# A decoder layer's out projection: two full token blocks first, the meta rows last

## The chip, the cores and the metric

One core of a Trainium2 chip runs one launch of the kernel. The metric is the device time of that launch in microseconds (us), median of several runs. Five engines work side by side and wait for each other by semaphores: PE (matrix products), DVE, ACT and POOL (elementwise work), and SP, which here only issues DMA transfers. Each engine takes its instructions in its own order; an instruction that waits holds up everything behind it on that engine.

## What is computed

One layer of a hybrid decoder on 1024 tokens and 16 meta rows put ahead of them, 1024 wide, all float32:

```python
a = rmsnorm(h, ln_mix_pre)                  # h = meta rows, then x
dq, dk, dv, hq, hf, hi, hg = split(a @ w_in)
y_diff = diff_attention(dq, dk, dv, ...)    # 4 heads
y_hgrn = hgrn2(hq, hf, hi, hg, ...)         # 4 heads, chunked recurrence
mix = concatenate([y_diff, y_hgrn]) @ w_out # the OUT PROJECTION, 1024 x 1024
h = h + rmsnorm(mix, ln_mix_post)
a = rmsnorm(h, ln_ffn_pre)
y = conv_ffn(a, w_ffn_up, ...)              # up, causal conv of width 3, gelu gate, down
h = h + rmsnorm(y, ln_ffn_post)
return h[16:]                               # the meta rows are dropped
```

Since the convolution looks back two rows, only the last two meta rows are needed behind the attention: "the meta rows" below are these two.

## The kernel before

Every float32 product is made of three products of rounded operands: each operand is split into a high part (a cast on ACT) and a low part (operand minus high part, on DVE or POOL), and PE adds high x high, high x low, low x high. So each step of the out projection is a group of three matmuls (`out_part`, L937, L939, L941).

**The out projection** is `mix @ w_out`. `mix` lies transposed in SBUF in eight pieces (k = 0 to 7) of 128 columns. The tokens are nine blocks: block 0 is the two meta rows (`tok(0)` gives 2 rows), blocks 1 to 8 have 128 each. `w_out` is taken in two halves of 512 columns: `load_wo(0)`, then `load_wo(1)`. A piece of a half is loaded as `wor` (256 KB, SP, L904) and split into `woh` (ACT) and `wol` (DVE or POOL).

*First half* (`out_first`, tags `py0_i`). PE runs it interleaved with the last HGRN head (`hgrn_head`), since the scores of that head give piece k = 7. `mix_split(i, k0, k1)` makes the parts of `mix` of block i in a tile `mm` (k 0 to 3 or 4 to 6), out of a pool `mixsplit` with two buffers a tag. It also writes the parts to a scratch tensor `msc` in DRAM (SP, L927), except for block 0. The half opens with blocks 0 and 1 in turn, two pieces of k each, goes on with block 2, and so on to 8; what PE sums is copied to `y0`. Piece k = 7 follows by itself when the head's rows are done (`out_last(p)`, PSUM tile `pz`): three matmuls, an add to `y0` on DVE, and the sum of squares of the row on ACT. ACT has to write the squares somewhere: for p < 3 they go into the PSUM tile `pz` itself. Blocks 0, 1, 2 get their `pz` at the end of `out_first`; 3 to 8 get it inside the second half, two behind each of its blocks 0, 1, 2.

*Second half* (the loop at the end, tags `py1_i`). The parts are not made again but read back from `msc` in four pieces of two k (`mix_load(i, c)`, tile `mp`, four buffers, 256 KB each, SP, L1001). Block 0 alone has no parts in `msc`: they are made anew from `mix` on ACT and DVE (four casts, four subtractions, L53). The order is block 0, 1, ..., 8. Behind each, `post(i, py)` adds the residual and makes the next norm, and two blocks later `trans(i)` transposes the rows on PE.

Three details matter. `gpo` and `gfb` are gain rows broadcast by SP (L1022, L1024), in a pool that is opened late. The **up weights** `ra` (`load_raw4`, L1106, 256 KB each, five buffers) are loaded for the next stage: `issue_after(wo0_loaded)` lets the scheduler put their issue anywhere behind the last load of the first half of `w_out`. Their splits `uh` (ACT), `ul` (POOL or DVE) and sums `ws` (POOL, L1110) follow. Last, every line of ACT and DVE of the helper that records the order is L53, so these are told apart by tiles.

Of the kernel before, what the change touches and what calls it, by code (L numbers as in the profile page):

```python
# [17 lines left out]
P = 128  # L18
# [8 lines left out]
NBLK = 9  # L27
# [58 lines left out]
def layer_kernel(ctx: ExitStack, tc: tile.TileContext, x, meta, table, lbl, gpre, gpost, win,  # L86
# [830 lines left out]

    def mix_split(pl, i, k0, k1):
        r, t0 = tok(i)
        m = pl.tile([P, 2, k1 - k0, P], F32R, tag="m1" if k1 - k0 == 1 else "mm", name=f"mm{i}_{k0}")  # L920
        src = mix(slice(k0, k1), t0, t0 + r)
        A.copy(m[:, 0, :, :r], src)
        V.tensor_tensor(m[:, 1, :, :r], src, m[:, 0, :, :r].bitcast(F32), op=ALU.subtract)
        if i:
            for c in range(k0 // 2, (k1 + 1) // 2):
                ka, kb = max(k0, 2 * c), min(k1, 2 * c + 2)
                SY.dma_start(msc[i, c][:, :, P * (ka - 2 * c):P * (kb - 2 * c)],  # L927
                             m[:, :, ka - k0:kb - k0].bitcast(F32).rearrange("p l k t -> p l (k t)"))
        return m, k0, k1, r
# [11 lines left out]
            T.matmul(py[:r], ml[:, j, :r], hi, start=False, stop=(last and k == k1 - 1))  # L941
            yield 216

    first_split = mix_split(map_, 0, 0, 4)
    wo0 = load_wo(0)
    wo0_loaded = last_load[-1]

    pre_last = {}

# [4 lines left out]
    def out_last(p):  # L954
        r = tok(p)[0]
        py = ps_in(f"pz{p}")
        yield from out_part(pre_last.pop(p), py, wo0, True, True)
        V.tensor_tensor(y0[:r, p], y0[:r, p], py[:r], op=ALU.add)
        junk = py if p < 3 else qp.tile([P, 512], F32, tag="junk", name=f"jz{p}", bufs=1)
        A.activation(junk[:r], y0[:r, p], AF.Square, accum_out=ssy[:r, p, 0:1])  # L960
        A.activation(ssy[:r, p, 0:1], ssy[:r, p, 0:1], AF.Identity, bias=eps[:r], scale=1.0 / D)
        if p < 3:
            y0_gain(p)

    def out_first():
        pys = [ps_in(f"py0_{i}") for i in range(2)]
        sps = [first_split, mix_split(map_, 1, 0, 4)]
        for ks in ((0, 1), (2, 3)):
            for i in range(2):
                yield from out_part(sps[i], pys[i], wo0, ks[0] == 0, False, ks)  # L970
        sqs = [mix_split(map_, i, 4, 7) for i in range(2)]
        for i in range(2):
            yield from out_part(sqs[i], pys[i], wo0, False, True)
            if i == 0:
                sp_ = mix_split(map_, 2, 0, 4)
            A.copy(y0[: tok(i)[0], i], pys[i][: tok(i)[0]])
        for i in range(2, NBLK):
            py = ps_in(f"py0_{i}")
            sq_ = mix_split(map_, i, 4, 7)
            yield from out_part(sp_, py, wo0, True, False)  # L980
            if i + 1 < NBLK:
                sp_ = mix_split(map_, i + 1, 0, 4)
            yield from out_part(sq_, py, wo0, False, True)
            (V.tensor_copy if i == NBLK - 1 else A.copy)(y0[: tok(i)[0], i], py[: tok(i)[0]])
        for p in range(3):
            while p not in finished:
                yield None
            if p < 2:
                for q in range(2 * p, min(2 * p + 2, 3)):
                    pre_last[q] = mix_split(map_, q, 7, 8)  # L990
            yield from out_last(p)
# [5 lines left out]
    def mix_load(i, c):  # L997
        r, t0 = tok(i)
        m = mlp.tile([P, 2, 2, P], F32R, tag="mp", name=f"mp{i}_{c}", bufs=4)
        if i:  # L1000
            SY.dma_start(m.bitcast(F32).rearrange("p l k t -> p l (k t)"), msc[i, c])  # L1001
        else:
            src = mix(slice(2 * c, 2 * c + 2), t0, t0 + r)
            A.copy(m[:, 0, :, :r], src)
            V.tensor_tensor(m[:, 1, :, :r], src, m[:, 0, :, :r].bitcast(F32), op=ALU.subtract)
# [21 lines left out]
    def post(i, py):  # L1027
        r, t0 = tok(i)
        xh = qp.tile([P, D], F32, tag="xh", name=f"xh{i}")
        SY.dma_start(xh[:r], meta[14:16, :] if i == 0 else x[P * (i - 1): P * i, :])  # L1030
        if i >= 3 and i % 2:
            a2 = mxp.tile([P, 8, 384], F32, tag="mix2", name=f"a2_{i}").rearrange("p a c -> p (a c)")[:, :D]
        else:
# [3 lines left out]
        s1, s2 = ssy[:r, i, 1:2], ssy[:r, i, 2:3]  # L1037
        A.activation(junk[:r], py[:r], AF.Square, accum_out=s1)
# [7 lines left out]
        A.activation(a2[:r], xh[:r], AF.Square, accum_out=s2)  # L1046
# [54 lines left out]
    def load_raw4(ft):  # L1101
        raws.clear()
        for nm, m, c in (("11", ft, 0), ("22", ft + NF, 1), ("21", ft + NF, 0), ("12", ft, 1)):
            raws[nm] = swp.tile([P, 512], F32, tag="ra", name=f"ra{ft}_{nm}", bufs=5)
            with tc.issue_after(wo0_loaded.ins):
                SY.dma_start(raws[nm], wup[m][:, 512 * c: 512 * (c + 1)])  # L1106

    def w_sum(nm, a, b, op):
# [38 lines left out]
            split(hi, lo, raws[nm], G)  # L1147
            plain[nm] = (hi, lo)

    ms = [mix_load(0, c) for c in range(4)]  # L1150
    for i in range(NBLK):
        py = ps_s(f"py1_{i}")[:, 0]
        if i == NBLK - 1:
            prep_plain()
        if i >= 3:
            y0_gain(i)
        nxt = []
        for c in range(4):
            if c == 2:
                if i < 3:  # L1160
                    for p in (3 + 2 * i, 4 + 2 * i):
# [15 lines left out]
        if i < 3:  # L1177
            for p in (3 + 2 * i, 4 + 2 * i):
                for _ in out_last(p):
                    pass  # L1180
    close(q_cm, ma_cm, y_cm, wo_cm)
# [368 lines left out]
```

## Time and profile before

| | |
|---|---|
| median of 3 runs (1350.4 to 1353.11) | 1351.55 us |
| the profiled execution | 1350.57 us |
| its span, first to last instruction | 1348.7 us |
| PE busy | 1297.8 us, 96% of the span |
| DVE, ACT, POOL busy | 927.7, 687.3, 422.1 us |
| mean granted clock of PE | 0.993 |
| first half of the out projection | 528.69 to 595.84 us |
| k = 7 parts and second half | 595.84 to about 669 us |

The profiled execution is 0.98 us under the median, and 1.87 us of it lie outside the span. Rows of the trace give the start in us from the span's first instruction, the duration, the engine, the line, out<-in, and in brackets how long the engine had been idle and what released it. "Waits" sums such idle time by what was waited for. PEclk is the share of the full TensorE clock that was granted.

### The profile page before, as it was taken

Reading aid. Unit: us, or ns where it says so; the run is one execution under the profiler, and the core shown is the slowest. Engines: PE = TensorE matmul, PEld = TensorE weight load, DVE = VectorE, ACT = ScalarE, POOL = GpSimd, SP = SyncE. Lnnn points to the kernel's source line nnn. Section 1 sums busy time; section 2 is a strip of 40 time slices with the busy share of each in tenths; the row PEclk is TensorE's granted clock in tenths of the full one; section 3 lists DMA queues with packets and bytes.
Section 4 is the critical chain, followed back from the end, with each engine's and each line's share of the span. In section 5 each row is a group of like instructions: output and inputs, shape, how many; then the busy total and the mean of one; then the engine's idle time right before and its main releaser. Section 6 shows DMA issues by size and latency. Waiting matters only on the chain.

```text
span 1348.7 us, 26259 instructions
## 1 busy us (share of the span) xinstructions
PE 1297.8 (96%) x10170; PEld 1187.0 (88%) x10170; DVE 927.7 (69%) x1599; ACT 687.3 (51%) x1629; POOL 422.1 (31%) x334
## 2 busy tenths in 40 slices
PE   6999999999999999989999999999999999999997
PEld 5899899989999997667798999999999998878875
DVE  7665657574746464756798787787777776697586
ACT  7465346534644664455674444444454444554453
POOL 3211211021112110234036656656656640010121
PEclk9999999999999999999999999999999999999999
DMA  6331333132311002648712222223222225955253
GB/s 213 113 126 52 103 126 102 44 127 102 103 44 42 26 23 85 218 145 261 262 40 87 94 87 72 79 88 102 79 87 78 72 89 185 339 186 169 87 203 117
DMA packets 87028, 157.01 MB, mean 116 GB/s; under 512 B 9796, under 2 KB 24164, under 8 KB 86903
## 3 DMA queue, kind: packets, MB, share of 16 engines
q1 hardware_dynamic: 86902, 155.33, 34.2%
q8 instruction: 80, 1.31, 0.4%
q14 instruction: 46, 0.37, 0.1%
HBM read 114.66 MB, written 40.63 MB: 115 GB/s over the span
## 4 chain that ended last, share of the span: by engine, by line
PE 69%; DVE 6%; DMA 4%; issue 3%; ACT 3%; POOL 1%; SPq 0%; DVEq 0%; ACTq 0%; POOLq 0%
PE pd L1396 5%; PE pd L1397 5%; PE pd L1395 5%; PE pb L1237 4%; PE pb L1239 4%; PE pb L1238 4%; PE pc L1237 3%; PE pc L1239 2%; PE pc L1238 2%; PE pa L1237 2%; PE pa L1238 2%; PE pa L1239 2%; PE pa L694 2%; PE py L937 2%; PE py L941 2%
## 5 line engine op out<-in xcount | busy, mean ns | idle before, releaser
L1237 PE MATMUL pb<-t,uh 128*128 128x258 f32 x504 | 143.5, 285 | 4.7 <-DVE u L53 4.7
L1239 PE MATMUL pb<-t,ul 128*128 128x258 f32 x504 | 141.7, 281 | 0.0
L1238 PE MATMUL pb<-t,uh 128*128 128x258 f32 x504 | 141.6, 281 | 0.0
L1396 PE MATMUL pd<-wl,gh 128*128 128x512 f32 x308 | 122.0, 396 | 0.6 <-DVE wl L53 0.5
L1395 PE MATMUL pd<-wh,gh 128*128 128x512 f32 x308 | 121.7, 395 | 0.0
L1397 PE MATMUL pd<-wh,gl 128*128 128x512 f32 x308 | 121.6, 395 | 0.0
L53 DVE SCALAR_TENSOR_TENSOR c<-uu,cwt,c 128x514 f32<-128x514 f32 (+1 forms) x88 | 96.4, 1096 | 20.6 <-ACT c L53 19.9
L1204 POOL TENSOR_TENSOR c<-c,c 128x514 f32<-128x514 f32 (+1 forms) x44 | 63.4, 1441 | 122.8 <-ACT c L53 120.1
L1237 PEld LDWEIGHTS pb<-t,uh 128*128 128x128 f32 x504 | 94.9, 188 | 6.8 <-DVE u L53 6.2
L1239 PEld LDWEIGHTS pb<-t,ul 128*128 128x128 f32 x504 | 95.2, 189 | 0.0
L1238 PEld LDWEIGHTS pb<-t,uh 128*128 128x128 f32 x504 | 95.2, 189 | 0.0
L1238 PE MATMUL pc<-t,uh 128*128 128x258 f32 (+1 forms) x336 | 95.1, 283 | 0.0
L1237 PE MATMUL pc<-t,uh 128*128 128x258 f32 (+1 forms) x336 | 95.0, 283 | 0.0
L1239 PE MATMUL pc<-t,ul 128*128 128x258 f32 (+1 forms) x336 | 95.0, 283 | 0.0
L1237 PE MATMUL pa<-t,uh 128*128 128x258 f32 (+1 forms) x336 | 94.8, 282 | 0.0
L1238 PE MATMUL pa<-t,uh 128*128 128x258 f32 (+1 forms) x336 | 94.6, 281 | 0.0
L1239 PE MATMUL pa<-t,ul 128*128 128x258 f32 (+1 forms) x336 | 94.2, 280 | 0.0
L53 DVE SCALAR_TENSOR_TENSOR c<-ug,cwt,c 128x514 f32<-128x514 f32 (+1 forms) x88 | 86.1, 978 | 2.7 <-ACT c L53 2.0
L145 POOL TENSOR_TENSOR ul<-ws,uh 128x512 fp32r<-128x512 f32 x42 | 60.0, 1428 | 42.9 <-ACT uh L53 38.7
L1396 PEld LDWEIGHTS pd<-wl,gh 128*128 128x128 f32 x308 | 57.7, 187 | 15.9 <-DVE wl L53 1.9
L1397 PEld LDWEIGHTS pd<-wh,gl 128*128 128x128 f32 x308 | 57.7, 187 | 14.1
L1395 PEld LDWEIGHTS pd<-wh,gh 128*128 128x128 f32 x308 | 57.7, 187 | 14.0
(343 smaller groups left out, 4145.5 us busy)
## 6 DMA issues: line engine op xcount, KB each, us to landing
ra<-in_wup_dram SPq DMA_DIRECT2D x88, 256.0 KB, 2.6
wd<-in_wdown_dram SPq DMA_DIRECT2D x44, 256.0 KB, 4.4
tsc<-wd SPq DMA_DIRECT2D x44, 256.0 KB, 2.9
wi<-tsc SPq DMA_DIRECT2D x44, 256.0 KB, 3.0
gi<-gsc SPq DMA_DIRECT2D x33, 256.0 KB, 3.8
wi<-in_wdown_dram SPq DMA_DIRECT2D x33, 256.0 KB, 3.5
mp<-msc SPq DMA_DIRECT2D x32, 256.0 KB, 3.7
msc<-mm SPq DMA_DIRECT2D x24, 256.0 KB, 2.5
```

Of the source, the lines that this page charges most:

```text
L53: ins = call(*args, **kw)
L145: (eng or G).tensor_tensor(lo, raw, hi.bitcast(F32), op=ALU.subtract)
L694: T.matmul(po[:, :P], w_, vn[:, j], start=(j == 0), stop=(j == i))
L937: T.matmul(py[:r], mh[:, j, :r], hi, start=(first and j == 0), stop=False)
L941: T.matmul(py[:r], ml[:, j, :r], hi, start=False, stop=(last and k == k1 - 1))
L1204: G.tensor_tensor(cg, cg, cu, op=ALU.mult)
L1237: T.matmul(pt, hi[:, s], th[:, k], start=(first and k == 0), stop=False, skip_group_check=True)
L1238: T.matmul(pt, hi[:, s], tl[:, k], start=False, stop=False, skip_group_check=True)
L1239: T.matmul(pt, lo[:, s], th[:, k], start=False, stop=(k == 3), skip_group_check=True)
L1395: T.matmul(py, gh[:, s], wh, start=(k == 0 and pr not in (3, 7)), stop=False, skip_group_check=True)
L1396: T.matmul(py, gh[:, s], wl, start=False, stop=False, skip_group_check=True)
L1397: T.matmul(py, gl[:, s], wh, start=False, stop=(k == NH - 1), skip_group_check=True)
```

## The change

In words, in program order:

- the pool of parts `mixsplit` has three buffers a tag in place of two (`m1` keeps two);
- the parts of the meta rows get a tile of their own, `m0`, for all eight k. They are made once (k 0 to 6 at the start, k = 7 with its `pz`), and `mix_load` no longer makes them anew;
- the first half opens on blocks 1 and 2 in turn; block 0 comes last, behind block 8 (`out_meta`, k 0 to 6);
- the last copy of a block to `y0` is on ACT, no longer on DVE;
- the squares of `out_last` for p < 3 go to a tile in SBUF, out of `mixsplit`, not into `pz`;
- the second half takes 1, 0, 2, 3, ..., 8, with the `pz` of 3 to 8 behind blocks 1, 2, 3 (two each); four `mp` loads of block 1 stand ahead of the loop;
- the up weights are loaded behind the last load of the **second** half of `w_out` (`wo1_loaded`);
- `post(0)` works in other tiles (its squares in PSUM, its row in place).

```diff
-    ma_cm, map_ = pool("mixsplit", 2)
+    ma_cm, map_ = pool("mixsplit", 3)
+    m0 = yp.tile([P, 2, KD, 2], F32R, tag="m0", name="m0")
...
     def mix_split(pl, i, k0, k1):
+        if i == 0:
+            m = m0[:, :, k0:k1]
...
+    def out_meta(py, wo, nk):
+        return out_part((m0, 0, nk, 2), py, wo, True, True)
+
+    sps = [mix_split(map_, i, 0, 4) for i in (1, 2)]
+    mix_split(map_, 0, 0, 7)
     wo0 = load_wo(0)
-    wo0_loaded = last_load[-1]
...
-        junk = py if p < 3 else qp.tile([P, 512], F32, tag="junk", name=f"jz{p}", bufs=1)
+        junk = (map_ if p < 3 else qp).tile([P, 512], F32, tag="junk", name=f"jz{p}", bufs=1)
...
-            (V.tensor_copy if i == NBLK - 1 else A.copy)(y0[: tok(i)[0], i], py[: tok(i)[0]])
+            A.copy(y0[:, i], py)
+        py = ps_in("py0_0")
+        yield from out_meta(py, wo0, 7)
+        A.copy(y0[:2, 0], py[:2])
...
     wo = load_wo(1)
+    wo1_loaded = last_load[-1]
...
-            with tc.issue_after(wo0_loaded.ins):
+            with tc.issue_after(wo1_loaded.ins):
                 SY.dma_start(raws[nm], wup[m][:, 512 * c: 512 * (c + 1)])
...
-    ms = [mix_load(0, c) for c in range(4)]
-    for i in range(NBLK):
+    order = (1, 0, 2, 3, 4, 5, 6, 7, 8)
+    ms = [mix_load(1, c) for c in range(4)]
+    for i in order:
+        py = ps_s(f"py1_{i}")
...
+        if i == 0:
+            for _ in out_meta(py[:, 0], wo, KD):
+                pass
+            post(i, py)
+            continue
```

Where instructions stand on an engine, before and after, is told by the following pieces of the program's order.

The first is ACT's order where the first half opens. `sg` are the three steps of the last HGRN gate, `mm_0` the high parts of k 0 to 3 of a block, `woh` those of `w_out`. Before:

```order
L53 ACTIVATE sg_2_6281<-pi_hg_2_6256 128x384
L53 CAST mm_0_6302<-mix_94 128x4x2
L53 CAST woh_2_6319<-wor_2_6317 128x512
L53 ACTIVATE sg_2_6281<-sg_2_6281,one 128x384
L53 CAST woh_3_6325<-wor_3_6323 128x512
L53 ACTIVATE sg_2_6281<-sg_2_6281 128x384
L53 CAST woh_4_6331<-wor_4_6329 128x512
L53 CAST mm_0_6355<-mix_94 128x512
L53 CAST woh_5_6337<-wor_5_6335 128x512
```

And with the change (`m` is the tile `m0`, k 0 to 6 of the meta rows):

```order
L53 ACTIVATE sg_2_6281<-pi_hg_2_6256 128x384
L53 CAST mm_0_6303<-mix_94 128x512
L53 ACTIVATE sg_2_6281<-sg_2_6281,one 128x384
L53 CAST mm_0_6308<-mix_94 128x512
L53 ACTIVATE sg_2_6281<-sg_2_6281 128x384
L53 CAST m_6299<-mix_94 128x14
L53 CAST woh_2_6329<-wor_2_6327 128x512
L53 CAST woh_3_6335<-wor_3_6333 128x512
L53 CAST woh_4_6341<-wor_4_6339 128x512
```

The casts of two full blocks now stand ahead of the weights `woh_2` to `woh_4`; the cast of block 1 stood behind them.

The second is SP's order at the junction of the halves. Before, two `ra` loads stand between the last loads of `w_out` and the parts of block 1 (`mp_0` to `mp_3`); seven others had been issued in the first half:

```order
L904 DMA wor_7_7120<-in_wout_dram 128x512
L927 DMA msc<-mm_7_7054 256x1x128
L1030 DMA xh_7205<-in_meta_dram 2x1024
L1030 DMA xh_7277<-in_x_dram 128x1024
L1106 DMA ra_22_8158<-in_wup_dram 128x512
L927 DMA msc<-mm_7_7181 256x1x128
L1001 DMA mp_0_7171<-msc 128x512
L927 DMA msc<-mm_7_7185 256x1x128
L1001 DMA mp_1_7179<-msc 128x512
```

With the change (L905 is L904 before, L1119 is L1106, L1029 and L1031 are L1022 and L1024, L1011 is L1001):

```order
L905 DMA wor_6_7113<-in_wout_dram 128x512
L905 DMA wor_7_7119<-in_wout_dram 128x512
L1119 DMA ra_11_7705<-in_wup_dram 128x512
L1119 DMA ra_22_7707<-in_wup_dram 128x512
L1119 DMA ra_21_7709<-in_wup_dram 128x512
L1119 DMA ra_12_7711<-in_wup_dram 128x512
L1119 DMA ra_11_7957<-in_wup_dram 128x512
L1119 DMA ra_22_7959<-in_wup_dram 128x512
L1029 DMA gpo<-in_gpost_dram 128x512
L1031 DMA gfb<-in_gfpre_dram 128x1024
L1011 DMA mp_0_7151<-msc 128x512
```

No `ra` is issued in the first half any more. Six stand in a row behind `wor_7`, then `gpo` and `gfb`, and only then `mp_0`. The sixth `ra` takes the first one's buffer again (five buffers): it waits for the last reader of that one, POOL's `ul` of `ra_11`. `gfb` waits for ACT's squares of block 2's `pz`.

The third is PE's order at the same place, three matmuls a group, of which one row is shown here for each piece. Before:

```order
L941 MATMUL pz_7046<-woh_7_6349,mm_7_7039 2x512
L941 MATMUL pz_7058<-woh_7_6349,mm_7_7042 128x512
L941 MATMUL pz_7066<-woh_7_6349,mm_7_7054 128x512
...
L941 MATMUL py_0_7164<-woh_0_7080,mp_0_7152 2x512
...
L941 MATMUL pz_7220<-woh_7_6349,mm_7_7181 128x512
L941 MATMUL pz_7228<-woh_7_6349,mm_7_7185 128x512
...
L941 MATMUL py_1_7236<-woh_0_7080,mp_0_7171 128x512
```

With the change (L947 is L941, and L943 is L937):

```order
L947 MATMUL pz_7042<-woh_7_6359,m_6299 2x512
L947 MATMUL pz_7055<-woh_7_6359,mm_7_7038 128x512
L947 MATMUL pz_7064<-woh_7_6359,mm_7_7051 128x512
...
L947 MATMUL py_1_7159<-woh_0_7079,mp_0_7151 128x512
...
L947 MATMUL pz_7216<-woh_7_6359,mm_7_7176 128x512
L947 MATMUL pz_7224<-woh_7_6359,mm_7_7180 128x512
L947 MATMUL py_0_7232<-woh_0_7079,m_6299 2x512
```

The 24 matmuls of the meta rows and the six of two `pz` stood between the first three `pz` and the first use of `mp` read from DRAM. They now stand behind block 1's 24.

More of the change, by code (lines that the diff above doesn't have):

```diff
@@ L965, in out_first @@
     def out_first():
-        pys = [ps_in(f"py0_{i}") for i in range(2)]
-        sps = [first_split, mix_split(map_, 1, 0, 4)]
+        pys = [ps_in(f"py0_{i}") for i in (1, 2)]
         for ks in ((0, 1), (2, 3)):
[L969 to L977, printed above, removed]
+            for j in range(2):
+                yield from out_part(sps[j], pys[j], wo0, ks[0] == 0, False, ks)
+        sqs = [mix_split(map_, i, 4, 7) for i in (1, 2)]
+        for j in range(2):
+            yield from out_part(sqs[j], pys[j], wo0, False, True)
+            if j == 0:
+                sp_ = mix_split(map_, 3, 0, 4)
+            A.copy(y0[:, 1 + j], pys[j])
+        for i in range(3, NBLK):
             py = ps_in(f"py0_{i}")
@@ L999, in mix_load @@
         m = mlp.tile([P, 2, 2, P], F32R, tag="mp", name=f"mp{i}_{c}", bufs=4)
[L1000 to L1005, printed above, removed]
+        SY.dma_start(m.bitcast(F32).rearrange("p l k t -> p l (k t)"), msc[i, c])
         return m, 2 * c, 2 * c + 2, r
     wo = load_wo(1)
+    wo1_loaded = last_load[-1]
     close(h_cm, at_p_cm)
@@ L1159, in layer_kernel @@
             if c == 2:
-                if i < 3:
-                    for p in (3 + 2 * i, 4 + 2 * i):
+                if i < 4:
+                    for p in (1 + 2 * i, 2 + 2 * i):
                         pre_last[p] = mix_split(mlp, p, 7, 8)
@@ L1176, in layer_kernel @@
             t_split(0, 6, quarter(0, 6), mxp, "mix1", 384)
-        if i < 3:
-            for p in (3 + 2 * i, 4 + 2 * i):
+        if i < 4:
+            for p in (1 + 2 * i, 2 + 2 * i):
                 for _ in out_last(p):
```

16 lines of the change are left out of this document (12 added, 4 removed).

## The prediction

> **What bounds the kernel now.** The table of busy time by stretch comes first. PE is busy 96% of the span (page, above), so time can only be gained where PE is idle or its clock is low. Its columns: stretch, length, then for each engine busy us and instructions, the granted clock, the share of DMA time, GB/s.
>
> ```profile
> 530.00:535.00 5.00, 3.35 (x11) 1.42 (x10) 3.55 (x6) 2.87 (x6) 0.00 (x0) 0.85 0.66 213
> 535.00:540.00 5.00, 5.00 (x81) 2.73 (x80) 2.75 (x8) 1.35 (x4) 0.00 (x0) 0.81 0.73 232
> 550.00:555.00 5.00, 3.61 (x75) 2.43 (x75) 2.60 (x5) 2.56 (x5) 2.91 (x6) 0.89 0.66 209
> 555.00:560.00 5.00, 5.00 (x81) 3.62 (x81) 5.00 (x12) 1.75 (x4) 2.32 (x2) 0.76 0.85 283
> 600.00:605.00 5.00, 2.04 (x6) 0.39 (x6) 4.53 (x7) 2.70 (x12) 4.92 (x4) 0.67 0.35 107
> 605.00:610.00 5.00, 5.00 (x16) 1.52 (x15) 3.66 (x4) 1.24 (x2) 4.92 (x4) 0.64 0.32 101
> 650.00:660.00 10.00, 8.85 (x47) 7.09 (x46) 4.91 (x7) 5.51 (x16) 0.00 (x0) 1.00 0.96 299
> ```
>
> Three places lose time: the opening (530 to 540), the middle of the first half (550 to 560), the junction of the halves (595 to 610). Each has idle PE and, behind it, a clock under 1.00. At 650 to 660 the clock is whole, but the DMA engines are busy 0.96 of the time: there transfers are the limit, not arithmetic. PE's waits from 515 to 705 say for whom it waits (us, times, longest):
>
> ```profile
> PE py L937 <- ACT mm L53: 2.9, 3, 1.4
> PE py L937 <- DMA mp<-msc: 1.9, 3, 1.2
> ...
> PE py L941 <- DVE mm L53: 1.0, 3, 0.6
> ```
>
> **The opening, before.** PE's timeline; the last of the HGRN projection, then the out projection:
>
> ```profile
> 527.69 0.33 PE L221 MATMUL pi_hg<-ahi,wl_hg 128*128 128x384 f32 x1
> 528.69 0.40 PE L937 MATMUL py<-woh,mm 128*2 128x512 f32 x1 [0.67 <-ACT mm L53]
> 528.92 0.39 PE L939 MATMUL py<-wol,mm 128*2 128x512 f32 x1
> 531.68 0.50 PE L937 MATMUL py<-woh,mm 128*128 128x512 f32 x1 [1.45 <-ACT mm L53]
> 532.62 0.50 PE L941 MATMUL py<-woh,mm 128*128 128x512 f32 x1 [0.20 <-DVE mm L53]
> 533.82 0.63 PE L937 MATMUL py<-woh,mm 128*2 128x512 f32 x1
> 534.25 0.63 PE L939 MATMUL py<-wol,mm 128*2 128x512 f32 x1
> ```
>
> A 512-column matmul takes a step of 0.23 us (528.69 to 528.92) at the whole clock and 0.43 (533.82 to 534.25) at the low one. Idle here is 0.67 + 1.45 + 0.20 = 2.32. The low clock costs 5 x (0.15 + 0.19) = 1.7 by the two stretches. So the opening loses 4.0.
>
> **The opening, after.** ACT's timeline before shows why PE stalls, and gives the durations:
>
> ```profile
> 528.45 0.19 ACT L53 CAST mm<-mix 128x8 fp32r<-128x8 f32 x1
> 531.01 0.62 ACT L53 CAST mm<-mix 128x512 fp32r<-128x512 f32 x1
> 532.28 0.62 ACT L53 CAST woh<-wor 128x512 fp32r<-128x512 f32 x1 [0.65 <-DMA wor<-in_wout_dram]
> ```
>
> With the change a full cast of 0.62 stands where the small one stood, at 528.45: the first matmul comes at about 529.1 instead of 528.69, 1.1 behind the end of the projection (527.69 + 0.33). The cast of the second block is done by about 530.2, and PE needs it after six matmuls, at 529.1 + 6 x 0.23 = 530.5. So the 1.45 goes; a wait of about 0.15 for DVE's subtraction stays. What is late next is the weights: the casts `woh_2` to `woh_4` move behind two full casts, `wol_2` gives its `wor` buffer free some 2.3 us later, and the load of `wor_5` leaves behind four writes of `msc` (1 MB). PE wants `woh_5` after some 27 matmuls, at 535.4. By these steps it lands at 535.8 to 536, and with cast and subtraction the stalls for k = 5 and 6 come to about 1.25. Bounds: nothing, or 2.3 with a low-clock stretch of 1.6 like the one above, 3.9. I take 1.9, since a gap of 1.45 was enough for the low clock in the rows above. The opening then loses 1.1 + 0.15 + 1.9 = 3.1: **0.9 gained** (bounds -1.1 to 2.8).
>
> **The middle.** The chain that ended last, at 546 to 554 (start, us, what):
>
> ```profile
> 546.78 4.37 DMA ra<-in_wup_dram
> 551.75 0.62 ACT mm L53
> 552.40 1.36 DVE mm L53
> ```
>
> An up weight's cast stands ahead of the parts of a block on ACT, and waits 4.37 us for its transfer; the cast of the parts queues behind it, PE behind both. PE idles 0.75 and 0.65 here by its timeline:
>
> ```profile
> 552.42 0.50 PE L937 MATMUL py<-woh,mm 128*128 128x512 f32 x1 [0.75 <-ACT mm L53]
> 553.80 0.69 PE L941 MATMUL py<-woh,mm 128*128 128x512 f32 x1 [0.65 <-DVE mm L53]
> ```
>
> The clock behind costs 5 x (0.11 + 0.24) = 1.75 by the stretches. With the change no `ra` is issued, cast or subtracted in the first half, and a third buffer lets the parts run a block ahead. What is late next there is PE itself, busy 5.00 of 5.00 at 555 to 560. **3.1 gained** (bounds 1.4, if the clock stays low, to 3.4). The third wait for DVE's `mm` (1.0 in all, less 0.20 and 0.6) should go as well, 0.2. First half together: 0.9 + 3.1 + 0.2 = **4.2**, bounds 0.3 to 6.4.
>
> **The junction, before.** PE's timeline from the first `pz` to the first block with parts from DRAM:
>
> ```profile
> 595.84 0.39 PE L937 MATMUL pz<-woh,mm 128*2 128x512 f32 x1
> 599.17 0.50 PE L937 MATMUL pz<-woh,mm 128*128 128x512 f32 x1 [1.06 <-ACT pz L53]
> 601.89 0.59 PE L937 MATMUL py<-woh,mp 128*2 128x512 f32 x1 [1.76 <-ACT mp L53]
> 604.10 0.59 PE L941 MATMUL py<-woh,mp 128*2 128x512 f32 x1 [1.20 <-DVE mp L53]
> 612.60 0.39 PE L937 MATMUL py<-woh,mp 128*128 128x512 f32 x1
> ```
>
> Between 595.84 and 612.60 lie 39 matmuls (nine and six of `pz`, 24 of the meta rows), 39 x 0.232 = 9.0 of work in 16.8. The waits named here go: squares in SBUF give the `pz` bank free at the add, and nothing is split here for the meta rows. But SP's timeline and waits show what these 16.8 us also hid:
>
> ```profile
> 606.91 0.33 SPq L1106 DMA_DIRECT2D ra<-in_wup_dram  x1
> 607.96 0.56 SPq L1001 DMA_DIRECT2D mp<-msc  x1
> ```
>
> ```profile
> SPq L1106 <- POOL ws L1110: 7.4, 1, 7.4
> ```
>
> SP stood 7.4 us at an `ra` load whose buffer POOL still read, and the first `mp` left 12.1 behind 595.84. The meta rows' matmuls needed no `mp`; they covered this.
>
> **The junction, after.** Call E the end of the first half's last matmul. PE has only nine matmuls of `pz` left, to E + 2.1, and then needs `mp_0`. SP's order puts six `ra`, `gpo` and `gfb` ahead of it, and the sixth `ra` waits for POOL's `ul` of the first. Durations from before:
>
> ```profile
> 598.40 0.59 ACT L53 ACTIVATE pz<-y 2x512 f32<-2x512 f32 x1
> 598.57 1.28 POOL L145 TENSOR_TENSOR ul<-ws,uh 128x512 fp32r<-128x512 f32 x1 [0.73 <-ACT uh L53]
> 599.80 2.49 POOL L952 TENSOR_TENSOR y<-y,gpo 2x512 f32<-2x512 f32 x2
> 602.25 1.77 POOL L145 TENSOR_TENSOR wol<-wor,woh 128x512 fp32r<-128x512 f32 x1
> ```
>
> These are a square, a split and two gains (1.25 each) on otherwise free rows, and a split beside a busy DVE. The transfers' medians from issue to landing, 590 to 625 us:
>
> ```profile
> mp<-msc SPq DMA_DIRECT2D x10, 256.0 KB, 3.7
> wor<-in_wout_dram SPq DMA_DIRECT2D x2, 256.0 KB, 4.8
> ```
>
> `wor_7` leaves when POOL has done `wol_4`, whose weight tile comes free with the meta rows' k = 3: about E + 0.1. With the 3.7 of the equally large `mp` it lands at E + 3.8 (with the 4.8 that the two `wor` took, at 4.9). ACT then casts it, squares a block (0.59) and casts `ra_11`, to about E + 5.9. POOL has before that `wol_6` and two gains, then `ul_11`, 1.28 to 1.77: done at about E + 7.5. SP then issues the sixth `ra`, `gpo`, `gfb` and `mp_0` at 0.33 to 0.56 each, so `mp_0` leaves at E + 9.0 and lands at **E + 12.7** (bounds 10, if the weights come sooner, and 14.5, with 4.8 for `wor` and 1.77 on POOL). PE idles 10.6; the low clock behind it I put at 2.6, between the 1.7 of the opening and the 3.4 of two such stretches. Then come the 30 matmuls that stood in front before, 7.0. So the same 39 matmuls take 12.7 + 2.6 + 7.0 = 22.3 instead of 16.8: **5.5 lost** (bounds 1.9 to 8.1).
>
> [...] The low clock followed 2.3 us of idle in pieces of at most 1.45, and 1.4 in pieces of 0.75 and 0.65. [...] I go by the rows.
>
> **The rest of the second half.** Its waits for `mp` sum to 1.9 (table above). Five `ra` of 256 KB now fall among its loads, at 0.26 MB / 290 GB/s = 0.9 each 4.5 of transfers, and the meta rows' 24 matmuls stand behind block 1 as cover, 5.6. I take 0.5 lost, bounds -1.5 to 2.5; without that cover it would be 4.5. The other edits (the last copy on ACT, `post(0)` in place, parts of the meta rows made once) are at most a few 0.6 us instructions on engines that are idle a third of the time; cover is PE's work, price nothing.
>
> **Sum.** -4.2 + 5.5 + 0.5 = +1.8 on the profiled execution's 1350.57 (1348.7 of span and 1.87 around): 1352.4. The median of the three runs is 0.98 above that execution, so the forecast for a median is **1353.3**.
>
> **The rivals.**
> *Faster: `mp_0` is early.* If POOL and ACT run their short rows (1.28, 0.59) without waiting and `mp_0` lands at E + 8.5, PE idles 6.4 and the junction takes 8.5 + 1.7 + 7.0 = 17.2, only 0.4 lost. With an opening stall of 1.25 the first half gains 4.9: -4.9 + 0.4 + 0.5 = -4.0, median 1347.5. For it: the DMA engines were busy 0.32 of the time at 605 to 610, so transfers can be quick. Against: every step of that chain waits for another engine. It decides from a landing before E + 10.
> *Slower: the block ahead of `mp_0` is longer.* One place, SP: with 4.8 for `wor_7` and 1.77 to 2.49 a step on POOL, `ul_11` is done at E + 9.3 and `mp_0` lands at E + 14.5; two low-clock stretches follow (3.4): 24.9 instead of 16.8, 8.1 lost. With the opening's stall at 3.4 the first half gains 2.7: -2.7 + 8.1 + 0.5 = +5.9, median 1357.4. For it: SP did stand 7.4 for POOL in the row above. Against: fewer POOL steps stand ahead here. It decides from a landing behind E + 13.5.
> *The clock does not follow short gaps.* 1.7 and 1.75 of low clock stay: +1.8 + 3.4 = +5.2, median 1356.8. Against: the low clock stands behind those gaps both times, and 650 to 660, with 1.15 idle, has 1.00.
> *The opening doesn't open sooner.* The weights stall it by as much as `mm` did: 0.9 less gain, median 1354.2.
>
> **How the numbers follow.** A measurement of this kernel tells about 0.2% (2.7 us) from no change. Chances: forecast 0.37 (its own range 1350.3 to 1356.3, from the bounds of its terms halved), `mp_0` early 0.26, longer block 0.22, clock 0.05, opening 0.10. Faster, under 1348.85: the first rival and a sliver of the forecast, 0.27. Slower, over 1354.25: the second and third rival (0.27), a third of the forecast (0.12) and half of the last (0.05), 0.44. Between: 0.29. The range takes in both outer rivals with some 2 us each for the unknown stalls: 1345.5 to 1359.
>
> **What would show it.** PE's wait for `ACT mm` near 551 gone, and the clock 1.00 there. In the opening, a wait for `woh` or `wol` in place of `ACT mm`. At the junction, one wait of PE for `mp<-msc` of about 10.6 us, SP waiting for POOL's `ul` just before, and a clock near 0.65 in the 5 us behind. The forecast is wrong if that wait is under 7 us, or if the first half gains less than 2.5.

## The result, and the profile after

| | before | changed |
|---|---|---|
| median us (runs) | 1352.33 (4) | 1368.99 (4: 1365.0 to 1371.76) |
| ratio | 1 | 1.0123, 95% interval 1.0094 to 1.0152 |
| profiled execution's span | 1348.7 | 1365.9 |

The change makes the kernel 16.7 us slower. The forecast was 1353.3, its range ended at 1359.

Both traces were cut at three points: the start of the last projection matmul, the first `pz`, and the first matmul of the next stage (`pq`). The stretches, in us:

| stretch | before | changed | difference | forecast |
|---|---|---|---|---|
| to the last projection matmul | 527.7 | 530.9 | +3.2 | 0 |
| first half of the out projection | 68.1 | 63.7 | -4.4 | -4.2 |
| first `pz` to next stage | 73.5 | 91.6 | +18.1 | +6.0 |
| the rest | 679.4 | 679.7 | +0.3 | 0 |

The first row is not the change's: the instructions of all engines stand in the same order up to there, and in the 16 profiles of this study that point lies anywhere from 527.7 to 533.4. So the kernels below are compared by the other three stretches, and by medians.

PE's waits from 515 to 720 us in the changed kernel (engine, line, waited for: us, times, longest):

```profile
PE py L943 <- DMA mp<-msc: 15.0, 3, 13.2
PE pa L1072 <- DVE xh L53: 8.5, 1, 8.5
PE py L943 <- ACT mm L53: 1.1, 1, 1.1
```

The waits for `ACT mp` and `DVE mp` are gone, and those for `ACT mm` fell from 2.9 to the 1.1 at the start, as forecast. Two long ones stand in their place: 13.2 for the first `mp` (forecast 10.6), and 8.5 at L1072, the transposes, of which the forecast says nothing. Both in PE's timeline:

```profile
594.56 0.40 PE L943 MATMUL pz<-woh,m 128*2 128x512 f32 x1
...
610.46 0.79 PE L943 MATMUL py<-woh,mp 128*128 128x512 f32 x1 [13.24 <-DMA mp<-msc]
617.93 0.40 PE L943 MATMUL pz<-woh,mm 128*128 128x512 f32 x1
...
627.43 0.40 PE L947 MATMUL py<-woh,mp 128*128 128x512 f32 x1
636.29 0.98 PE L1072 MATMUL pa<-ident,xh 2*128 2x2 f32 x8 [8.46 <-DVE xh L53]
```

E, the first `pz`, is 594.56; `mp` is used at E + 15.9. Block 1's 24 matmuls then take 7.5 (610.46 to 617.93) instead of 5.6 (24 matmuls at a whole clock took 5.64 before, 612.60 to 618.24). PE reaches the meta rows' transposes behind only twelve matmuls of block 2 and stands until 636.29. The table by stretch shows the clock (last but two columns) low behind both:

```profile
600.00:605.00 5.00, 0.00 (x0) 0.00 (x0) 5.00 (x1) 3.08 (x9) 5.00 (x5) 0.57 0.56 182
605.00:610.00 5.00, 0.00 (x0) 0.00 (x0) 3.17 (x4) 0.00 (x0) 1.61 (x2) 0.50 0.95 306
610.00:615.00 5.00, 4.54 (x12) 3.61 (x13) 0.00 (x0) 0.00 (x0) 0.00 (x0) 0.56 0.52 165
615.00:620.00 5.00, 5.00 (x23) 3.62 (x22) 1.15 (x2) 1.58 (x6) 0.00 (x0) 1.00 0.75 213
...
630.00:635.00 5.00, 0.00 (x0) 0.00 (x0) 3.23 (x3) 1.64 (x4) 4.76 (x4) 0.64 0.26 98
635.00:640.00 5.00, 3.71 (x15) 3.15 (x16) 1.14 (x1) 0.34 (x2) 0.07 (x1) 0.50 0.32 88
```

**Why `mp` came so late.** SP's timeline: `mp` left at 603.07, E + 8.5, half a microsecond before the forecast.

```profile
595.07 7.00 SPq L1119 DMA_DIRECT2D ra<-in_wup_dram  x6
602.17 0.38 SPq L1029 DMA_DIRECT2D gpo<-in_gpost_dram  x1
602.64 0.38 SPq L1031 DMA_DIRECT2D gfb<-in_gfpre_dram  x1
603.07 1.89 SPq L1011 DMA_DIRECT2D mp<-msc  x4
```

The transfer is what was mis-sized: 7.4 from its issue to the first use (603.07 to 610.46) instead of 3.7. The transfers of 600 to 612 us, with their medians to landing:

```profile
DMA packets 1770, 3.01 MB, mean 251 GB/s; under 512 B 172, under 2 KB 624, under 8 KB 1770
...
mp<-msc SPq DMA_DIRECT2D x4, 256.0 KB, 7.7
gfb<-in_gfpre_dram SPq DMA_DIRECT2D x1, 512.0 KB, 7.2
...
gpo<-in_gpost_dram SPq DMA_DIRECT2D x1, 256.0 KB, 3.6
```

`gpo`, `gfb` and four `mp` were issued within 2.8 us of each other, 1.8 MB. At 251 GB/s that is 7.2 us, an estimate that agrees with what `gfb` and `mp` took; `gpo`, the first of the batch, landed after 3.6. The median of 3.7 came from loads that had no such batch ahead: in the kernel before, the two gain rows had left SP ahead of E (595.84), and the first `mp` took 3.4. SP's timeline before:

```profile
590.07 0.61 SPq L1022 DMA_DIRECT2D gpo<-in_gpost_dram  x1
...
593.95 0.62 SPq L1024 DMA_DIRECT2D gfb<-in_gfpre_dram  x1
```

**Why the meta rows came so late.** DVE's timeline behind their sum, which PE ended at 624.87:

```profile
625.83 3.45 DVE L53 TENSOR_TENSOR ul<-ws,uh 128x512 fp32r<-128x512 f32 x2
629.20 0.67 DVE L53 TENSOR_TENSOR tmp<-py,gpo 2x512 f32<-2x512 f32 x1
629.80 1.14 DVE L53 SCALAR_TENSOR_TENSOR xh<-y,ssy,xh 2x512 f32<-2x512 f32 x1
630.86 1.74 DVE L53 SCALAR_TENSOR_TENSOR xh<-tmp,ssy,xh 2x512 f32<-2x512 f32 x1
634.38 1.77 DVE L53 SCALAR_TENSOR_TENSOR xh<-xh,ssy,gfb 2x1024 f32<-2x1024 f32 x1 [1.77 <-ACT ssy L53]
```

It takes 11.3 us from sum to last product. Two splits of up weights stand ahead of it on DVE (3.45), and DVE's second and third step for the meta rows take 1.14 and 1.74, beside a POOL busy 5.00 of 5.00 at 625 to 630 and 4.76 at 630 to 635; before, with POOL idle, they took 0.74 and 0.73. In the kernel before, the last product of the meta rows on DVE, and their transposes on PE:

```profile
616.43 2.20 DVE L53 SCALAR_TENSOR_TENSOR a<-xh,ssy,gfb 2x1024 f32<-2x1024 f32 x1
```

```profile
622.52 0.65 PE L1059 MATMUL pa<-ident,a 2*128 2x2 f32 x8
```

There PE ended the sum at 611.2 and came to the transposes at 622.5, 48 matmuls later: 11.3 of cover for a chain of 7.4. Now the cover is 2.8 and the chain 11.3. Of the 8.5 of waiting, the old chain would have left 4.6 (7.4 - 2.8) and its growth makes 3.9, as an estimate from these two traces. Sum of the stretch: junction 24.7 instead of 16.8 (30.3 from E to 624.87, less 5.6 of block 1), +7.9; transposes 8.5 and ten matmuls at 0.43 instead of 0.23, +10.5; all else -0.3.

**A third reading was possible**, and it became the main rival: DVE and POOL in each other's way. One subtraction took 8.94, where another of the same form (at 592.64) took 0.69; it ended at 607.16, 0.55 behind POOL's work without a pause (to 606.61). DVE's timeline, then the first and the last row of POOL's:

```profile
598.22 8.94 DVE L53 TENSOR_TENSOR wol<-wor,woh 128x512 fp32r<-128x512 f32 x1 [0.28 <-ACT woh L53]
```

```profile
598.01 2.48 POOL L961 TENSOR_TENSOR y<-y,gpo 2x512 f32<-2x512 f32 x2
...
602.91 3.70 POOL L145 TENSOR_TENSOR ul<-ra,uh 128x512 fp32r<-128x512 f32 x3
```

### The profile page after: what moved, and what is told of

Its sections match the earlier page's. It is cut to its first block, busy times and chain, and to the rows that moved or that the text cites. A ratio compares the mean times of both kernels' runs of the same rounds, so it can differ in the third digit from the quotient of the medians.

```text
span 1365.9 us, 26232 instructions
## 1 busy us (share of the span) xinstructions
PE 1296.2 (95%) x10170; PEld 1190.2 (87%) x10170; DVE 931.0 (68%) x1593; ACT 688.1 (50%) x1625; POOL 421.7 (31%) x334
## 4 chain that ended last, share of the span: by engine, by line
PE 45%; DVE 3%; issue 2%; DMA 1%; POOL 1%; ACT 1%; SPq 0%; DVEq 0%; POOLq 0%; ACTq 0%
PE pd L1416 5%; PE pd L1417 5%; PE pd L1415 5%; PE pb L1257 4%; PE pb L1259 4%; PE pb L1258 4%; PE pc L1257 3%; PE pc L1259 3%; PE pc L1258 3%; PE pa L1257 2%; PE pa L1258 2%; PE pa L1259 2%; DMA mp<-msc 1%; PE py L943 1%; PE py L947 1%
```

## Experiments

Each run's stretches are those of its one profiled execution; the medians are of 4 to 12 executions. The theory: two separate losses, the transposes too close behind the meta rows and `mp` behind the up weights and gain rows. The rival: POOL's up-weight work beside DVE is behind both. The stretches of all runs (first half; first `pz` to next stage; rest), and medians with the ratio to the kernel before in the same runs:

| run | first half | middle | rest | median | ratio (interval) |
|---|---|---|---|---|---|
| x1, transposes swapped | 63.2 | 85.7 | 678.1 | 1359.24 | 1.0056 (1.0037 to 1.0075) |
| x2, meta rows first | 63.2 | 82.2 | 683.3 | 1360.61 | 1.0067 (1.0051 to 1.0083) |
| x3, up weights early | 63.9 | 88.4 | 678.4 | 1364.62 | 1.0088 (1.0071 to 1.0106) |
| x4, up weights behind `mp` | 63.3 | 85.7 | 678.4 | 1359.38 | 1.0055 (1.0036 to 1.0073) |
| x5 = x1 + x4 | 63.1 | 81.0 | 678.4 | 1357.79 | 1.0049 (1.0032 to 1.0066) |
| x6 = x2 + x4 | 63.3 | 70.3 | 689.1 | 1357.7 | 1.0043 (1.0028 to 1.0058) |
| y1, before + third buffer | 67.5 | 77.2 | 678.5 | 1357.18 | 1.0046 (1.0028 to 1.0063) |
| y2, before + up weights late | 64.6 | 75.5 | 679.6 | 1351.71 | 0.9993 (0.9978 to 1.0008) |
| z1 = x2 + x3 | 64.5 | 79.4 | 679.1 | 1355.51 | 1.0014 (1.0 to 1.0028) |
| z2, see below | 63.5 | 71.4 | 687.4 | 1354.95 | 1.0019 (1.0007 to 1.003) |
| z3 = x2 + low parts on DVE | 62.8 | 82.4 | 682.3 | 1357.84 | 1.0031 (1.0017 to 1.0045) |
| z5, up weights divided | 63.9 | 75.3 | 682.2 | 1353.13 | 0.9999 (0.9984 to 1.0013) |
| z6 = z5, squares in PSUM | 64.6 | 74.4 | 680.2 | 1348.38 | 0.9967 (0.9948 to 0.9986) |
| w1, changed, squares in PSUM | 63.1 | 93.1 | 678.6 | 1366.07 | 1.01 (1.0071 to 1.013) |

### x1: the transposes swapped

```diff
-                    trans(i - 2)
+                    trans({2: 1, 3: 0}.get(i, i - 2))
```

> The changed kernel, with the transposes of block 1 made in block 2's turn and those of the meta rows one block later, in block 3's. Theory (the meta rows are post-processed too late for the transposes, which the new order puts 12 matmuls behind them): PE's wait for DVE's xh (8.5 us) and the low clock behind it (2.0) go, 9 to 10.5 us faster than the changed kernel, about 1359 us. Rival (DVE is held up by POOL as such; its backlog from 620 to 636 us is what counts): PE meets the backlog at the next place, under 4 us faster, 1365 or more.

PE's waits of 600 to 660:

```profile
PE py L943 <- DMA mp<-msc: 13.5, 1, 13.5
PE pa L1072 <- DVE a L53: 1.8, 1, 1.8
PE py L943 <- ACT py L53: 1.0, 1, 1.0
```

The wait for `xh` is gone, the wait for `mp` untouched. The median falls by 9.8, as the theory says, but by stretches only 5.9 of it is here (91.6 to 85.7); 2.1 and 1.6 of the profile's difference lie ahead of the first half and behind the middle, where the edit changes nothing; they are taken as scatter. New waits, 1.8 and 1.0 above among them, eat the rest. The close transposes are shown as one cause, of 6 to 10 us.

### x2 and x3: the meta rows first; the up weights early

```diff
-    order = (1, 0, 2, 3, 4, 5, 6, 7, 8)
+    order = (0, 1, 2, 3, 4, 5, 6, 7, 8)
```

> The changed kernel with its second half in the order 0, 1, 2 to 8, nothing else. Theory: the meta rows' 24 matmuls stand again between the pz and the first use of mp, and two blocks ahead of their transposes. The first mp still lands about 15.9 us behind E, of which 9 are covered: 6 to 7 us of the junction come back, and the 10.5 of the transposes: about 1352 us, the first half's gain of 4.7 being eaten by what is left of the idle junction. Rival (DVE and POOL in each other's way, wherever the meta rows stand): at least half of the loss stays, over 1359.

```diff
     wo0 = load_wo(0)
+    wo0_loaded = last_load[-1]
...
-            with tc.issue_after(wo1_loaded.ins):
+            with tc.issue_after(wo0_loaded.ins):
```

> The changed kernel with the up weights again behind the first half's last load of w_out. Theory: only two ra stand ahead of mp at the junction, the first mp lands about 9 to 10 us behind E instead of 15.9, 5 to 6 us come back there; the first half gives about 3 of its 4.7 back; the transposes' wait stays, since the order is the same: 1364 to 1368 us. Rival (it is POOL's work on the up weights that slows DVE): the transposes' wait goes too, 1357 or less.

x2 lands at 1360.6, just on the rival's side of 1359: 9.4 of the 18.1 come back in the middle stretch, and 3.6 of them are lost again in the rest (683.3 for 679.7). PE's waits of 515 to 710 now name DVE's long subtraction:

```profile
PE py L943 <- DMA mp<-msc: 5.3, 2, 3.2
PE py L945 <- DVE wol L53: 5.1, 2, 4.9
```

So DVE's long subtraction, 8.96 here, does hold PE up, by 4.9; in the changed kernel the longer wait for `mp` hid it. x3 gives the 1364.6 that the theory asks for, but for another reason: SP stands at an `ra` load again, `mp` leaves only at E + 11.2, and PE waits 15.4 for it, 2.2 more than in the changed kernel.

```profile
SPq L1120 <- POOL ws L1124: 8.8, 1, 8.8
```

What came back is at the transposes, whose wait was to stay and fell from 8.5 to 3.1: with the up weights split earlier, less stands ahead of the meta rows. The first half, 63.9, did not give its gain back, against my expectation.

### x4 and x5: the up weights behind `mp`; both mended

```diff
+        ld = SY.dma_start(...)          # in mix_load
+        if i == 1:
+            mp_loaded.append(ld)
...
-            with tc.issue_after(wo1_loaded.ins):
+            with tc.issue_after(mp_loaded[-1].ins):
```

> The changed kernel with the up weights issued behind the four mp loads of block 1. Theory: nothing but gpo and gfb stands ahead of mp at the junction, the first mp lands 8 to 10 us behind E, 6 to 8 us come back; the transposes' wait stays or grows, as the up weights' sums then fall beside the meta rows: 1360 to 1366 us. Rival (the junction's wait is the transfer itself, slow in a full queue, not its late issue): the first mp still lands over 13 us behind E, 1367 or more.

PE's timeline of x4:

```profile
604.87 0.79 PE L943 MATMUL py<-woh,mp 128*128 128x512 f32 x1 [8.25 <-DMA mp<-msc]
627.19 0.98 PE L1076 MATMUL pa<-ident,xh 2*128 2x2 f32 x8 [4.99 <-DVE xh L53]
```

E is 594.0 here: `mp` is used at E + 10.9 instead of 15.9. Of these 5.0, 2.8 are the earlier issue (599.69, E + 5.7 for E + 8.5) and 2.2 the shorter transfer (5.2 for 7.4). So the up weights ahead of `mp` are worth 5 us at the junction. The transposes' wait, which was to stay or grow, fell by 3.5, and the median, 1359.4, lies just under the 1360 to 1366 expected.

x5 is x1 and x4 together.

> The changed kernel with both edits: the transposes of blocks 1 and 0 swapped, and the up weights issued behind the mp loads of block 1. Theory (two separate losses, a late mp at the junction and a late meta row at the transposes): the gains of 9.8 and 9.6 us add up, about 1350 us. Rival (both edits mend the same thing, POOL's up-weight work beside DVE): the gains overlap, 1355 or more.

It came to 1357.8, by the rival's number (1355 or more). By medians the gains overlap: 9.8 and 9.6 alone, 11.2 together. By the middle stretch they nearly add up: 5.9 and 5.9 alone, 10.6 together. So x5 does not decide between theory and rival. What stays in its middle stretch (81.0, 7.5 over before) shows in PE's waits of 515 to 705:

```profile
PE py L943 <- DMA mp<-msc: 12.7, 3, 8.0
```

The 8.0 are at the junction, where the meta rows no longer cover the load; 4.4 more are at a later block's `mp`. No wait for `xh` is left.

### x6: meta rows first, up weights behind `mp`

Both edits above (x2 and x4).

> The changed kernel with the second half in the order 0, 1, 2 to 8 and the up weights behind the mp loads of block 1. Theory: the first half keeps its gain of 4.5, the first mp lands about 11 us behind E, nine of them covered by the pz and the meta rows; DVE finds POOL idle there; the junction takes 11 to 12 us instead of 16.8 before: 1343 to 1346 us, faster than the kernel before. Rival (the up weights, pushed among the second half's loads, cost there what they give at the junction): 1350 or more.

The middle stretch is 70.3, 3.2 shorter than before, with the first half 63.3. By that 1344 was in reach. But the rest takes 689.1 instead of 679.4. PE's waits of 655 to 760:

```profile
PE pb L1261 <- DVE u L53: 7.3, 3, 3.3
PE pq L1243 <- DVE t L53: 2.5, 1, 2.5
...
PE pq L1244 <- POOL ul L145: 1.4, 1, 1.4
PE pq L1242 <- ACT ug L53: 1.4, 1, 1.4
```

The next stage waits for its operands: what the late loads save here is owed there, at waits for DVE, POOL and ACT. The rival's number came (1350 or more), but it had put the cost among the second half's loads. x5, with the same late loads, has no such cost behind its longer middle stretch (678.4); middle and rest together are 759.4 in both.

### y1 and y2: what made the first half shorter

y1 gives the kernel before a third buffer of parts (k = 7 keeps two), y2 only moves its up weights.

```diff
-    ma_cm, map_ = pool("mixsplit", 2)
+    ma_cm, map_ = pool("mixsplit", 3)
```

> The kernel before with a third buffer for the parts (k = 7 keeps two), nothing else. Theory (the buffers make the middle of the first half smooth, as the run with the up weights early has no stall there either): the first half from the last projection matmul to the first pz takes 65 us instead of 68.1, the opening as before. Rival (the prediction's step: the up weight's cast ahead of the parts on ACT is the cause): the stall of 1.4 idle and 1.75 of low clock near 552 stays, 67.5 us or more.

```diff
     wo = load_wo(1)
+    wo1_loaded = last_load[-1]
...
-            with tc.issue_after(wo0_loaded.ins):
+            with tc.issue_after(wo1_loaded.ins):
```

> The kernel before with the up weights behind the last load of the second half of w_out, nothing else. The prediction's step: the stall near 552 goes, the first half takes about 65 us; one ra stands ahead of mp at the junction and the meta rows cover: no loss there. Rival (two buffers stall the parts with or without the up weights): 67.5 us or more in the first half; and the up weights' work may cost over 2 us in the second half either way.

y1 keeps a stall in the middle, in a new place; PE's timeline:

```profile
559.52 1.05 PE L436 MATMUL pl<-mix,kr 128*32 128x16 f32 x64 [3.35 <-DVE mix L53]
```

ACT's cast of an up weight had waited 7.4 us for its load just ahead. y2 has no such stall and a first half of 64.6. So in the kernel before it is the up weight's cast, as predicted. The sizes are less clear. In y1 and y2 the opening, which neither edit touches, ran at a granted clock of 1.00, and in the one trace of the kernel before at 0.85 and 0.81, a difference that the prediction priced at 1.7. By that estimate y2's 3.5 become 1.8, and y1's 0.6 becomes a loss of 1.1: buffers alone gave nothing. And x3 shows that with the new opening and three buffers the early up weights do no harm (63.9). So the first half is short with late up weights (y2), and also with the new opening and three buffers (x3).

As a whole y2 is unchanged (0.9993; its middle stretch is 2.0 longer) and y1 is slower (1.0046; middle 77.2). Why y1's middle is longer stays open.

### z3: was DVE held up by POOL?

x2 with `split(hi, lo, raws[nm], V)` in place of `G` in `prep_plain`.

> The run with the order 0, 1, 2 to 8 alone, with the low parts of the first four up weights on DVE instead of POOL. Theory (DVE's subtraction for the last piece of w_out took 8.96 us because POOL worked without a pause): it takes under 2.5 us, PE's wait for it (4.9) goes, and SP waits less for the sixth up weight: from the first pz to the next stage 76 to 79 us instead of 82.2. Rival (DVE was waiting for something else): the subtraction stays above 5 us, the stretch above 81.

```profile
595.26 1.37 DVE L53 TENSOR_TENSOR wol<-wor,woh 128x512 fp32r<-128x512 f32 x1 [0.45 <-ACT woh L53]
```

The subtraction takes 1.37 instead of 8.96 with those splits off POOL. But POOL works without a pause beside it here too, from 593.53 to 599.48, so its unbroken work alone does not make the 8.96. And the stretch stays at 82.4, as the rival had it: at the junction PE now waits 7.1 for `mp` instead of 4.9 for DVE and 2.1 for `mp`. The long subtraction was not the bound.

### z1, z2, z5, z6, w1: a version that gives something

z1 is x2 and x3. z2 has the meta rows first, the first four up weights behind `w_out` and the others behind `mp`, `gpo` and `gfb` behind `mp` too, and `prep_plain`'s low parts on DVE.

> The changed kernel with its second half in the order 0, 1, 2 to 8 and the up weights behind the first half's w_out, so that of the change the new opening, the three buffers, the parts made once and the squares in SBUF are left. Theory (those parts give the first half's 4 us, the two moves take all that is lost): first half 63.5 to 64 us, from the first pz to the next stage 73 to 76, the rest as before: 1348 to 1351 us. Rival (the squares in SBUF or the lack of parts to split let the junction wait elsewhere): that stretch takes over 78 us, 1353 or more.

> The changed kernel with the order 0, 1, 2 to 8, the first four up weights behind w_out and the others behind the mp loads of block 1, gpo and gfb behind these too, and the low parts of the first four on DVE. Theory: mp leaves SP with no wait for POOL or ACT ahead of it, DVE is not held up by POOL, and the up weights are ready for the next stage: from the first pz to the next stage 69 to 72 us, the rest 679 to 682: 1343 to 1348 us. Rival (the up weights are late for the next stage as they were with all of them behind mp): the rest takes 685 us or more, no gain over the kernel before.

z1 missed, by the rival's numbers: the median is 1355.5 and the middle 79.4, so with the order and the up weights both put back 5.9 of the 18.1 are still there. SP waits 8.9 for POOL at an `ra` ahead of `mp`, much as it did before (7.4), but now `gpo` and `gfb` stand between that `ra` and `mp`, and PE waits 10.1 for `mp`. z2 has the good middle (71.4) and pays in the rest (687.4), as x6 did and as its rival had it.

z5 has the meta rows first too and divides the up weights; the first two groups, eight loads, go early as before, the others behind `mp`:

```diff
-            with tc.issue_after(wo1_loaded.ins):
+            with tc.issue_after((wo0_loaded if ft < 2 else mp_loaded[-1]).ins):
```

> The changed kernel with the order 0, 1, 2 to 8, the first eight up weights behind the first half's w_out (as before) and the others behind the mp loads of block 1. Theory: nothing but gpo and gfb stands ahead of mp at the junction, and the up weights for the first units are split early as in the kernel before. First half 63.5 to 64.5 us, from the first pz to the next stage 70 to 73, the rest 679 to 681: 4 to 7 us faster than the kernel before. Rival (what is won at the junction is owed by the next stage, whatever the order of the loads, since DVE and POOL have the same work to do): the rest takes 685 us or more, within 2 us of the kernel before.

No gain: 0.9999, though the rest (682.2) is not the 685 of the rival. SP's longest new wait of 585 to 680 says why, and PE's timeline what it cost:

```profile
SPq L1036 <- ACT jz L53: 5.4, 1, 5.4
```

```profile
608.13 0.80 PE L943 MATMUL py<-woh,mp 128*128 128x512 f32 x1 [5.47 <-DMA mp<-msc]
```

`gfb` waits for ACT's squares. The change had put them into a tile of `mixsplit`, and `gfb`, in a pool opened later, takes that place. z6 puts them back into PSUM, and w1 does so in the changed kernel.

```diff
-        junk = (map_ if p < 3 else qp).tile([P, 512], F32, tag="junk", name=f"jz{p}", bufs=1)
+        junk = py if p < 3 else qp.tile([P, 512], F32, tag="junk", name=f"jz{p}", bufs=1)
```

> The run with the up weights divided (order 0, 1, 2 to 8; eight early, the others behind mp) with the squares of the first three pz back in PSUM. Theory (the squares' tile in SBUF lies where gfb goes, so that gfb, ahead of mp on SP, waits 5.4 us for ACT): gfb and mp leave 4 to 5 us earlier, PE's wait of 5.5 for the first mp shrinks to under 2 even with 1 us more for the third pz: from the first pz to the next stage 70 to 73 us instead of 75.3, 2 to 5 us faster than the kernel before. Rival (the transfers, not their issue, are the limit there): the stretch stays over 74.5, within 1 us of the run before it.

> The changed kernel with the squares of the first three pz back in PSUM, nothing else. Theory (in the changed kernel mp waits behind the sixth up weight, which comes later than the squares): the first mp still leaves SP 8 to 9 us behind E, 1367 to 1371 us, as the changed kernel. Rival (the squares' tile is what makes the junction long there too): 1364 or less.

z6, PE's timeline:

```profile
597.92 0.59 PE L943 MATMUL pz<-woh,mm 128*128 128x512 f32 x1 [2.08 <-ACT pz L53]
606.34 0.50 PE L943 MATMUL py<-woh,mp 128*128 128x512 f32 x1 [0.35 <-DMA mp<-msc]
```

The wait for `mp` is 0.35 instead of 5.47, for 2.1 more at the third `pz`. z6 is the one version here whose interval lies under the kernel before, 0.9967 (0.9948 to 0.9986): some 4.5 us by the ratio, 3.5 by the medians (1348.4 for 1351.9). What the gain is made of is not shown. Six of its twelve executions took 1343.8 to 1346.5 us, the other six 1350.2 to 1355.1, and the profiled one (1350.6) is of the second six and no faster than the profile of the kernel before (1350.57). Its first half is 3.5 shorter than in that profile, whose low clock in the opening is 1.7 of it. Its middle, 74.4, missed the 70 to 73 expected and is only 0.9 under z5's, since PE now waits 4.8 for the transposes' rows: the rival's 74.5 was as near.

w1, PE's timeline:

```profile
604.29 0.80 PE L943 MATMUL py<-woh,mp 128*128 128x512 f32 x1 [7.85 <-DMA mp<-msc]
634.19 0.98 PE L1072 MATMUL pa<-ident,xh 2*128 2x2 f32 x8 [11.54 <-DVE xh L53]
```

In time the theory's bound nearly holds (1366.1), but its reason fell: in w1 only four `ra` stand ahead of `mp`, which leaves at E + 4.8 and is used at E + 11.6, 4.3 earlier. The meta rows' sum ends at E + 27.0, 3.3 earlier. The transposes wait 3 us longer instead. They start at E + 41.5, in the changed kernel at E + 41.7. So when the meta rows are ready did not follow from when PE summed them. The up weights' splits and sums stand among their steps on ACT, DVE and POOL; which of the three engines sets the time, no run shows.

## Why the prediction was wrong

- **The opening** (0.9 gained) and **the middle of the first half** (3.1): right together, 4.4 measured for 4.2, but in part by luck. The stall for `woh_5` was 0.42 and 0.23, not 1.9; the start's 1.09 as forecast. With 0.32 for DVE the opening lost 2.1 instead of 3.1, at a whole clock, so it gave some 1.9 and left 2.5 for the middle. And 1.7 of the gain is the low clock of the one trace before, which y1 and y2 do not have with that same opening. The cause given for the middle stands for the kernel before (y2), though in the changed kernel the new opening and the buffers would have done it too (x3).
- **The junction, after** (5.5 lost): the chain on SP was right, `mp` left at E + 8.5 for E + 9.0. The landing was mis-sized, 7.4 for 3.7: a median of loads that stood apart was used for a load behind 0.77 MB and beside 0.77 more. The low clock behind it cost 1.9 (7.5 less 5.6), where 2.6 was put. The term is 7.9, near its bound of 8.1. x4 shows that 5 us of it are the up weights' place.
- **The rest of the second half** (0.5 lost, bounds -1.5 to 2.5): this step failed, 10.5 measured. I counted the meta rows' matmuls behind block 1 as cover for loads and did not ask who waits for their result. `trans(0)` stayed where it was, inside block 2's turn, so 48 matmuls between sum and transposes became twelve. x1 shows it: with the transposes one block later the wait is gone. The same step took the up weights' work as DMA time alone. Their work on ACT, DVE and POOL stands ahead of the meta rows' post-processing, whose chain took 11.3 us instead of 7.4; that it makes the chain long fits x3 and x4, where the transposes' wait falls to 3.1 and 5.0 with nothing but the loads of the up weights moved.
- **Edits costed at nothing**: the squares in SBUF were counted as a gain alone, at the third `pz`, and were not free. They hold `gfb`, and `mp` behind it, for 5.4 us in z5. In the changed kernel they cost nothing that shows: the middle stretch is 91.6 with them and 93.1 without, since the transposes then wait longer. But z1 keeps 5.9 of the 18.1 with the order and the up weights both put back, so the other edits have a share in the loss that the sum left out.
- **The rivals**: the longer block ahead of `mp` has the junction's size right (8.1) by another cause: it let SP be late, and it was the transfer that took long. No rival has the transposes. The clock's rival did not come, since the clock is 1.00 in every stretch from 530 to 595, but y1 and y2 bear out its ground, that the clock need not follow short gaps: it is 1.00 behind the same gaps there.

What stays open: the split of the 8.5 into 4.6 of position and 3.9 of the up weights' queue is worked out from the two traces, and no run shows it by itself. w1, where the sum comes 3.3 earlier and the transposes only 0.2, speaks against a chain of fixed length. Whether the two losses are one or two stays open too: x5 reads one way by its median and the other by its stretches. z3 speaks against the rival's reason, since a subtraction of 1.37 instead of 8.96 on DVE gave nothing in that stretch (82.4 for 82.2); but x3 and x4 show that the up weights' loads alone change both waits.

## What to carry over

When a block's turn is moved, follow it to its consumers as well: who waits for its result, how many instructions lay between, and what else is queued ahead of its post-processing on each engine. A wait behind which another stands nearly ready gives back little when it is mended: w1 moved it to the transposes, x6 into the next stage. For a transfer's landing, count the bytes issued just ahead of it and beside it, and divide by the rate in that stretch; here that gave 7.2 for a measured 7.4.

## What the hardware showed

**Equal short gaps, unequal clocks.** y2 opens with the same gaps as the kernel before (0.67, 1.45 and 0.2), and so does y1. PE's timeline in y2 and the clock (last but two columns) of the stretches behind:

```profile
531.57 0.40 PE L937 MATMUL py<-woh,mm 128*2 128x512 f32 x1 [0.67 <-ACT mm L53]
534.56 0.50 PE L937 MATMUL py<-woh,mm 128*128 128x512 f32 x1 [1.45 <-ACT mm L53]
```

```profile
530.00:535.00 5.00, 2.89 (x14) 1.30 (x12) 3.04 (x7) 3.57 (x8) 0.00 (x0) 1.00 0.34 105
535.00:540.00 5.00, 4.79 (x84) 2.90 (x83) 3.51 (x8) 1.98 (x4) 0.00 (x0) 1.00 0.86 261
```

Before, the clock was 0.85 and 0.81 there; in y1 it was 1.00 in both. So the 1.7 of low clock that the prediction took from that one trace was not a fixed price. Three gaps of 2.3 us in all, the longest 1.45, stood ahead of a clock of 0.85 and 0.81 in the trace before, and ahead of 1.00 in y1 and y2. What decides between the two, no run shows.

**DVE's subtraction beside POOL, long or short.** One subtraction of two SBUF operands took 8.94 us in the changed kernel, 8.96 in x2 and 4.01 in x4, and each time ended 0.55 or 0.56 behind a row of POOL's instructions without a pause. In the changed kernel that row is seven instructions from 598.01 to 606.61, with DVE's on record from 598.22. But in x1 the same subtraction took 1.50 inside such a row (594.09 to 604.91), and in z3 1.37 (593.53 to 599.48). So POOL's work without a pause is not enough for the long one; what else it takes, no run shows.
